# Two layers of a diffusion backbone: modulation weights requested on another queue, and a set order for norms and weight splits at the seam to the second layer

## The chip, the core and the metric

The kernel runs on one core of a Trainium2 chip. A core has five engines that work side by side, each through its own instructions in order: TensorE multiplies matrices (PE in the profile; its weight loads are PEld), VectorE (DVE) and ScalarE (ACT) work on elements, GpSimd (POOL) and SyncE (SP) here mostly request transfers between the chip's memory and the core's. A transfer is requested by an engine, in that engine's order, and moves on that engine's queue; sixteen DMA engines carry all queues. If an engine has to wait before it may request a transfer, because the buffer is still in use, what it would do next waits too.

The metric is the time of one execution on the device, in microseconds (us). Three runs of the kernel before gave 1735.34 to 1737.92 us, with a median of 1735.86.

## What is computed

Two layers work on 512 latent tokens and 256 context tokens of width 1024. Each layer modulates its normed input by six vectors that come from a conditioning vector c through a weight matrix, once for the latent and once for the context tokens:

```python
mx = jnp.split(c_act @ ada_w[i] + ada_b[i], 6, axis=-1)      # six vectors of 1024, layer i
h_x = modulate(rms_norm(x, norm1_g[i]), mx[0], mx[1])        # h * (1 + scale) + shift
# layer 0: windowed attention with a sink;  layer 1: retention in both directions
x = x + mx[2] * out_x
x = x + mx[5] * swiglu(modulate(rms_norm(x, norm2_g[i]), mx[3], mx[4]), ffn_w_in[i], ffn_w_out[i])
```

Here `swiglu` is `(silu(gate) * up) @ w_out` with a hidden width of 2816. The output is the latent stream. All data are float32; a product in that precision is made of three faster ones, from operands that are split into a high and a low part.

## The kernel before

**Splits.** Every operand of a product is split: ScalarE casts it to the high part (line L171), VectorE subtracts that from the operand to get the low part (L172). TensorE then does high by high, low by high and high by low. So each weight tile of 512 KB passes through one load, one cast of ScalarE and one subtraction of VectorE before TensorE can use it.

**Modulation tiles.** The six vectors of layer 1 aren't computed on TensorE. Each of 48 tiles of the transposed modulation weights (512 KB, buffer `adaw`, one buffer for layer 1) is loaded by `ada_load` (request at L275), multiplied with the row of c on VectorE and summed (`ada_tile`, L284; one such instruction for latent tokens alone, two where the context tokens need the vector too). `ada_next` does a tile and then requests the next, which therefore waits until VectorE is done with the buffer. Layer 1's tiles are requested by GpSimd, those eight of layer 0 that are handled so by SyncE (with three buffers).

**Layer 0's feed-forward part, gate and up.** From about 398 to 724 us, `seven(pos)` handles one of 20 blocks of 128 hidden units: seven products of 12 matmuls each by a scheme that saves an eighth product. SyncE requests the weights (`load_up` L1138 and L1139, `load_gate` L1134, `load_sum` L1143). After every second block `pair_sums` combines the activations and GpSimd stores them (`saved`, L1069 and L1071). GpSimd also requests transfers that add one part of a weight matrix to another in the chip's memory (`sum_add`, L830; `fo_sum`); `sum_copy` (L827, SyncE) comes before it. From block 5 on, two tiles are handled per block by `ada_next`, as the first and the third of the block's `jobs`.

**Layer 0's feed-forward part, output.** From about 724 to 889 us, seven products of six steps each (`FO`, 41 steps that TensorE does, the last two joined). Step i does 24 matmuls with two hidden blocks (12 in a product's last step). At its begin, `fo_split_weights(i + 2)` and `fo_split_tokens(i + 2)` split the operands of two steps later, and `fo_load(i + 3)` requests tokens (`op` from `saved`, L1227, 384 KB) and weights (`wraw` from `wfo` or `fo_sum`, L1234, 512 KB); three raw weight buffers go round, and three pairs of split ones. After a product `fo_add` (L1280) adds its sums to the streams. In the first five products, every even step ends with `ada_next`, for the 14 tiles that are left. In the last two products, squares for the next layer's norm are summed (`add_squares`, `context_square`, L1298; `context_total`, L1303), and in the last one `latent_norm` makes the first half of the latent tokens' normed input: per tile a multiply on VectorE (L1352), a cast with shift on ScalarE (L1355), and a low part on VectorE (L1356).

**Order.** In these two stages the order on all five engines is the program's, written by hand (`tc.manual_schedule`). From there on, in retention, a planner orders the work by its dependencies and costs; there `first_weights_v` requested and split the first two value weights (L1496, L171, L172), which `values_first` multiplies with the first half of the normed tokens (L1572), with `totals` between two halves of that product.

Of the kernel before, what the change touches and what calls it, by code (L numbers as in the profile page):

```python
# [54 lines left out]
def dit_kernel(ctx, tc, xT, cT, crow, small, consts, masks, tabs0, tabs1, jtab, adaQ, adaN, adaT, wst, wgu, wfo, out):  # L55
# [11 lines left out]
    def T(pool, cols, tag, bufs, dt=F32):  # L67
        return pool.tile([P, cols], dt, tag=tag, bufs=bufs, name=tag)
# [29 lines left out]
    def after(ins, others):  # L98
        for o in others if not by_hand[0] else ():
            tc.add_manual_dep(ins.ins, o.ins.name, order, reason="table set turn")  # L100
# [69 lines left out]
    def split(t, hi, lo, behind=()):  # L170
        after(nc.scalar.copy(hi, t), behind)  # L171
        return nc.vector.tensor_tensor(lo, t, hi, op=sub)  # L172
# [99 lines left out]

    def ada_load(l, part, d, room):
        w = T(room, 1024, "adaw", 1 if l else 3)
        (nc.gpsimd if l else nc.sync).dma_start(w, adaT[l, part * 8 + d])  # L275
        return w

    def ada_tile(l, part, d, streams, cr, behind, room, w=None):
# [970 lines left out]
    def fo_step(i, o, first, joined=False):  # L1249
        parts_, end = [], [fo.pop(j) for j in ((i, i + 1) if joined else (i,))]  # L1250
        k = 2 * FO[i][1]
        for x, w in end:
            n = x[0].shape[1] // 384
            for j in range(n):
                parts_.append((k, [t[:, j * 384:(j + 1) * 384] for t in x], w, j * 512))
                k += 1

        def one(k, xs, w, c, d):
            ws = slice(c + d * P, c + (d + 1) * P)
            for e, (p, r) in enumerate(((w[0], xs[0]), (w[1], xs[0]), (w[0], xs[1]))):  # L1260
                nc.tensor.matmul(o[d], p[:, ws], r, start=first and k + e == 0,  # L1261
                                 stop=k == PAIRS - 1 and e == 2, skip_group_check=True)

        if joined:
            for d in range(4):
                for part in parts_:
                    one(*part, d)
        else:
            for part in parts_:
                for d in range(4):  # L1270
                    one(*part, d)
# [71 lines left out]
    def first_quarters(k, half):  # L1343
        if k < 4:
            return h_first[k][:, 0:SC], h_first[k][:, SC:2 * SC]
        return [a[:, HALVES[half]] for a in h_rest[k - 4]]

    def latent_norm(half, ks, behind=()):
        b, y, c = mods[1, 0], ssq[0], HALVES[half]
        for k in ks:  # L1350
            t = hm[k][:, c]
            after(nc.vector.scalar_tensor_tensor(t, xr[k][:, c], acol[1, 0, 0][:, k:k + 1], y[:, c], mult, mult), behind)  # L1352
            if k > 3 or half == 0:
                hi, lo = first_quarters(k, half)
                nc.scalar.activation(hi, t, AF.Identity, bias=b[:, 0, k:k + 1])  # L1355
                nc.vector.scalar_tensor_tensor(lo, t, b[:, 0, k:k + 1], hi, add, sub)  # L1356

    def first_rms():
        tot = pj(SC)
# [13 lines left out]
    def late_sums(step):  # L1373
        if step < 2:
            add_squares(T0, (4 + 2 * step, 5 + 2 * step))
            for d in (4 + 2 * step, 5 + 2 * step):
                context_square(d, t_hn(SC))
        if step == 1:
            ctx_sum.append(pj(SC))
            context_total((4, 5), 4, 3)  # L1380
            first_rms()
        if step == 2:
            context_total((6, 7), 4, 3)
        if 0 < step < 5:
            latent_norm(0, (2 * step - 2, 2 * step - 1))

    def last_squares():
        y, c = ssq[0], slice(384, SX)
        for d in range(4):
            t = t_hn(512) if d < 2 else t_sq(512)  # L1390
            context_square(d, t[:, 0:SC])
            sq = t[:, SC:SC + P]
            nc.scalar.activation(sq, xr[d][:, c], AF.Square)
            nc.vector.tensor_tensor(y[:, c], y[:, c], sq, op=add)

    def nothing():
        pass
# [9 lines left out]
    def gates_negated():  # L1407
        ends.pop(0)()
        for s in range(2):
            nc.vector.tensor_scalar(mods[0, s][:, 0], mods[0, s][:, 5], -1.0, None, op0=mult)  # L1410

    row_t = []
    Hand = {mybir.EngineType.PE, mybir.EngineType.DVE, mybir.EngineType.Activation, mybir.EngineType.SP,
            mybir.EngineType.Pool}
    with tc.manual_schedule(engines=Hand):
        by_hand[0] = True
        for pos in range(2, FT):
            jobs = [nothing] * 3
            if pos == 2:
                jobs = [last_sum, gates_negated, nothing]  # L1420
            elif pos == 3:
                jobs[0] = rows_begin
            elif pos == 4:
                jobs[2] = rows_silu
                ada_ahead()
            else:
                cr = row_t[0]
                jobs[0] = jobs[2] = ada_next
            if pos == FT - 1:
                def begin():  # L1430
                    fo_split_weights(0)
                    fo_split_tokens(0)
                    fo_split_tokens(1)
                jobs[1] = begin
            end = seven(pos, jobs)
            for st in sum_turns.get(100 + pos, ()):
                st(None)
        fo_y = [bank("Y"), bank("Z"), bank("Z"), bank("Y")]
        o = fo_y
        for i, (prod, m) in enumerate(FO):  # L1440
            if m == 0 and prod:
                o = fo_y if prod in (2, 4) else fo_z if prod == 5 else [bank("X"), bank("X"), pj(384), pj(384)] \
                    if prod in (1, 3) else [bank("Y"), bank("Z"), bank("Z"), bank("Y")]
                if prod == 3:
                    fo_z = o
            if i == 0:
                fo_split_weights(1)
                last_gate(FT - 1)
            if i + 2 < len(FO):
                fo_split_weights(i + 2)  # L1450
                fo_split_tokens(i + 2)
                fo_load(i + 3)
            last = prod == 6 and m == (PAIRS - 3) // 2
            if i + 1 < len(FO) or last:
                fo_step(i, o, prod in (0, 1, 3, 6), last)
            if m == (PAIRS - 1) // 2:
                for args in (((0, 0),), ((0, 0),), ((4, 0, True),), ((4, 1),), ((4, 1, True), (0, 1)), ((4, 0),), ())[prod]:
                    fo_add(o, *args)
            if prod < 5:
                ada_next() if m % 2 == 0 and ada_q else None  # L1460
            elif prod == 5:
                early_sums(m)
            else:
                late_sums(m)
            if i == 2:
                Q.close()
                H = ExitStack()
                hpool[0] = H.enter_context(tc.tile_pool(name="hR", bufs=1, reuse_waits="tile", side="right"))
                h_rest += [(T(hpool[0], 512, "aq", 11, F32R), T(hpool[0], 512, "aq", 11, F32R)) for _ in range(4)]
                h_first += [T(hpool[0], 512, "aq", 11, F32R) for _ in range(3)]  # L1470
                off_grid(hpool[0], 16)
                h_first.insert(0, T(hpool[0], 512, "aq0", 1, F32R))
                hm += [T(hpool[0], 512, "qk", 8) for _ in range(KT)]
        fo_add(o, 0, 1)
        last_squares()
        by_hand[0] = False
    assert not ada_q
    F.close()
# [10 lines left out]
    hpool[1] = qp  # L1489
    off_grid(qp, 48)  # L1490
    h_sum = [(T(hS, 512, "sA", 16, F32R), T(hS, 512, "sA", 16, F32R)) for _ in range(KT)]
    chunk_base = wpos[0]

    def chunk(i, own=False):
        raw = T(qw, 1024, "wx", 4) if own else T(rp, 1024, "wraw", 2)
        nc.sync.dma_start(raw, wst[i])  # L1496
        return raw

    def add_chunk(raw, i):
        nc.gpsimd.dma_start(raw, wst[i], accum_op=add)  # L1500

    def split_chunk(raw, behind=()):
        w = w_parts(hpool[0])
        last_split[0] = split(raw, *w, behind)
        return w

    last_split, rope_end, rope_sum, other_sums = [None], [None], [None], []

    def t_qk(dt=F32R):
        return T(hpool[0], 512, "qk", 8, dt)  # L1510

# [125 lines left out]
        product_v(c, context_half(0), w, True)  # L1637
        return c

    wsel[0] = 2  # L1640
    b11 = first_weights_v(0)
    ends = []

    def totals():
# [8 lines left out]
    for hd in range(RH):  # L1653
# [2 lines left out]

        def other_values():

            b21 = [split_chunk(chunk(bv + i)) for i in (2, 3)]
            Xv = [W4("X"), W4("X")]  # L1660
            product_v(Xv, quarter_of("12"), b21, True)
            for t in range(2):
                nc.vector.tensor_tensor(vt[t], vt[t], Xv[t], op=add)
            c = cv if hd else context_values(b11)
            product_v(c, context_half(1), b21, False)
            vt.extend((T(rp, 512, "y0", 1), T(qp, 512, "vc", 1)))
            for t in range(2):
                nc.scalar.copy(vt[4 + t], c[t])
# [595 lines left out]
```

## Time and profile before

| | |
|---|---|
| median of 3 runs | 1735.86 us |
| profiled execution, whole time | 1735.32 us |
| its span, first to last instruction | 1733.2 us |
| mean granted TensorE clock | 0.991 |
| TensorE busy | 1685.6 us, 97% |
| VectorE busy | 1343.0 us, 77% |
| 48 tiles of layer 1, requested on GpSimd's queue | 512 KB each, median 4.0 us from request to landing |
| 8 tiles of layer 0, requested on SyncE's queue | 512 KB each, median 3.7 us |

A row of waits has the waiting engine, its tile and line, an arrow to what it waited for, and then the sum in us, the count and the longest. A row of instructions has its start, its length, engine, line, operation, written and read tiles with partitions and elements, and in brackets the idle time before it with what ended that. Rows of transfers have size and the time from request to landing. The clock is the share of full speed that TensorE was granted.

### The profile page before, as it was taken

Reading aid. Unit: us, or ns where it says so; the run is one execution under the profiler, and the core shown is the slowest. Engines: PE = TensorE matmul, PEld = TensorE weight load, DVE = VectorE, ACT = ScalarE, POOL = GpSimd, SP = SyncE. Lnnn points to the kernel's source line nnn. Section 1 sums busy time; section 2 is a strip of 40 time slices with the busy share of each in tenths; the row PEclk is TensorE's granted clock in tenths of the full one; section 3 lists DMA queues with packets and bytes.
Section 4 is the critical chain, followed back from the end, with each engine's and each line's share of the span. In section 5 each row is a group of like instructions: output and inputs, shape, how many; then the busy total and the mean of one; then the engine's idle time right before and its main releaser. Section 6 shows DMA issues by size and latency. Waiting matters only on the chain.

```text
span 1733.2 us, 27880 instructions
## 1 busy us (share of the span) xinstructions
PE 1685.6 (97%) x10798; PEld 1527.1 (88%) x10798; DVE 1343.0 (77%) x2395; ACT 895.0 (52%) x1565; POOL 116.2 (7%) x246
## 2 busy tenths in 40 slices
PE   8999999999989899999989999999999999999999
PEld 5878878899979899999978888888898899989998
DVE  6788888797768778877779866767757898876874
ACT  5578878474433343444565534534525565444442
POOL 0011111000111211200000000000000000000000
PEclk9999999999999999999999999999999999999999
DMA  9848967645766775798662644625624323333322
GB/s 384 310 90 188 238 145 192 212 152 173 218 211 227 226 234 197 273 314 288 234 176 62 183 110 100 189 65 125 193 62 110 122 74 107 114 109 107 102 86 85
DMA packets 113316, 293.87 MB, mean 170 GB/s; under 512 B 9520, under 2 KB 20288, under 8 KB 112928
## 3 DMA queue, kind: packets, MB, share of 16 engines
q1 hardware_dynamic: 87696, 218.75, 38.0%
q0 software_dynamic: 25200, 72.82, 17.7%
q8 instruction: 84, 1.38, 0.3%
q10 hardware_dynamic: 288, 0.52, 0.1%
q14 instruction: 48, 0.39, 0.1%
HBM read 274.82 MB, written 61.28 MB: 194 GB/s over the span
## 4 chain that ended last, share of the span: by engine, by line
PE 79%; DVE 8%; DMA 7%; ACT 3%; issue 2%; POOL 0%; SPq 0%; DVEq 0%; ACTq 0%
PE Y L971 13%; PE Z L1572 7%; PE Z L971 7%; PE pj L154 4%; PE pj L156 4%; PE pj L155 4%; PE X L971 3%; PE Y L1561 3%; DMA adaw<-in_adaT_dram 3%; PE S L727 2%; PE pT L753 2%; PE pO L775 2%; DVE wlo L172 2%; PE Z L1261 2%; PE Y L1261 2%; PE pj L1261 2%
## 5 line engine op out<-in xcount | busy, mean ns | idle before, releaser
L171 ACT CAST whi<-wraw 128x1024 fp32r<-128x1024 f32 (+1 forms) x285 | 295.8, 1042 | 303.1 <-PE Y L971 70.5
L172 DVE TENSOR_TENSOR wlo<-wraw,whi 128x1024 fp32r<-128x1024 f32 (+1 forms) x285 | 343.8, 1210 | 113.8 <-ACT whi L171 112.5
L971 PE MATMUL Y<-aq,whi 128*128 128x384 f32 x640 | 176.7, 342 | 0.0
L971 PE MATMUL Y<-aq,wlo 128*128 128x384 f32 x320 | 110.1, 344 | 19.9 <-DVE wlo L172 19.9
L971 PEld LDWEIGHTS Y<-aq,whi 128*128 128x128 f32 x640 | 120.0, 193 | 0.0
L284 DVE CUSTOM_DVE_ANT_0 y<-adaw,crow,small_sb 128x1024 bf16<-128x1024 f32 x64 | 82.1, 1283 | 45.7 <-DMA adaw<-in_adaT_dram 45.1
L1572 PE MATMUL Z<-whi,sA 128*128 128x512 f32 x256 | 80.7, 391 | 0.0
L971 PEld LDWEIGHTS Y<-aq,wlo 128*128 128x128 f32 x320 | 61.9, 194 | 21.1 <-DVE wlo L172 21.1
L108 ACT ACTIVATE pr<-pr,stat,qs 128x513 f32<-128x513 f32 (+2 forms) x96 | 74.3, 777 | 11.1 <-DVE stat L734 11.0
L154 PE MATMUL pj<-ax,whi 128*128 128x512 f32 x176 | 69.3, 394 | 0.7 <-DVE res L263 0.4
L156 PE MATMUL pj<-ax,whi 128*128 128x512 f32 x176 | 68.8, 391 | 0.0
L155 PE MATMUL pj<-ax,wlo 128*128 128x512 f32 x176 | 68.7, 390 | 0.0
L753 PE MATMUL pT<-const_sb,pr 128*128 128x128 f32 x352 | 56.4, 285 | 2.3 <-DVE pr L744 1.1
L263 DVE SCALAR_TENSOR_TENSOR res<-pj,mod,res 128x512 f32<-128x512 f32 (+1 forms) x64 | 45.3, 714 | 16.7 <-PE pj L156 16.7
L971 PE MATMUL Y<-sA,whi 128*128 128x256 f32 x304 | 58.1, 277 | 0.0
L728 DVE CUSTOM_DVE_ANT_0 pr<-S,mask,qs 128x256 f32<-128x256 f32 (+1 forms) x96 | 53.4, 568 | 5.4 <-PE S L727 4.4
L1572 PEld LDWEIGHTS Z<-whi,sA 128*128 128x128 f32 x256 | 48.0, 188 | 10.3
L971 PE MATMUL Y<-hx,whi 128*128 128x256 f32 x304 | 56.3, 277 | 0.0
L1261 PE MATMUL Y<-aq,whi 128*128 128x384 f32 x176 | 53.2, 338 | 2.0 <-ACT aq L171 2.0
L1572 PE MATMUL Z<-wlo,sA 128*128 128x512 f32 x128 | 50.5, 395 | 1.3 <-DVE wlo L172 1.3
L1261 PE MATMUL Z<-aq,whi 128*128 128x384 f32 x176 | 51.4, 334 | 0.0
L753 PEld LDWEIGHTS pT<-const_sb,pr 128*128 128x128 f32 x352 | 41.2, 145 | 11.2 <-issue 4.3
(598 smaller groups left out, 5102.6 us busy)
## 6 DMA issues: line engine op xcount, KB each, us to landing
wraw<-in_wst_dram SPq DMA_DIRECT2D x158, 512.0 KB, 3.7
adaw<-in_adaT_dram POOLq DMA_DIRECT2D x48, 512.0 KB, 4.0
op<-saved SPq DMA_DIRECT2D x35, 384.0 KB, 5.4
saved<-op POOLq DMA_DIRECT2D x33, 384.0 KB, 6.4
wraw<-in_wgu_dram SPq DMA_DIRECT2D x24, 512.0 KB, 4.5
gu_sum<-in_wgu_dram SPq DMA_DIRECT2D x8, 1280.0 KB, 12.7
gu_sum<-in_wgu_dram POOLq DMA_DIRECT2D x8, 1280.0 KB, 12.7
wraw<-fo_sum SPq DMA_DIRECT2D x20, 512.0 KB, 4.9
```

The lines of the kernel that those rows point to most:

```text
L108: ins = nc.scalar.activation(*args, **kw)
L154: nc.tensor.matmul(o, whi, xhi, start=first, stop=False)
L155: nc.tensor.matmul(o, wlo, xhi, start=False, stop=False)
L156: return nc.tensor.matmul(o, whi, xlo, start=False, stop=last)
L171: after(nc.scalar.copy(hi, t), behind)
L172: return nc.vector.tensor_tensor(lo, t, hi, op=sub)
L284: res.append(nc.vector.tensor_tensor_reduce(junk, w, cr[:, s * 1024:(s + 1) * 1024], 1.0, sm_t[:, C_ADAB + l * 48 + j:C_ADAB + l * 48 + j ...
L728: nc.vector.tensor_tensor_reduce(pt[:, c0:c0 + w], bank, mask[:, m0:m0 + w], 1.0, top, add, ALU.min, lo)
L753: nc.tensor.transpose(tp[:, a * P:(a + 1) * P], self.pr[(0, 2, 1, 3)[a]][:, ki * P:(ki + 1) * P], ident)
L971: nc.tensor.matmul(o, p, r, start=first and k + i == 0, stop=k == 3 and i == 2, skip_group_check=not first)
L1261: nc.tensor.matmul(o[d], p[:, ws], r, start=first and k + e == 0, stop=k == PAIRS - 1 and e == 2, skip_group_check=True)
L1572: ins = nc.tensor.matmul(os[t], p, r, start=first and k + i == 0, stop=k == 3 and i == 2, skip_group_check=by_k or not first)
```

## The change

Three things change; what is computed stays the same.

1. `ada_load` requests all tiles on SyncE's queue. In the program's order those 48 requests now stand among SyncE's loads.
2. In the last product, `latent_norm` begins a step later and takes three, three and two tiles in steps 2, 3 and 4 instead of two in each of steps 1 to 4. Within a group all multiplies come first, then all shifts on ScalarE, then all low parts.
3. Retention's first two value weights are requested and split inside the hand order: the first split before the last `fo_add`, the second after `last_squares`. The next two are ordered behind the last of these squares. The helpers `chunk`, `add_chunk` and `split_chunk` move up unchanged.

```diff
     def ada_load(l, part, d, room):
         w = T(room, 1024, "adaw", 1 if l else 3)
-        (nc.gpsimd if l else nc.sync).dma_start(w, adaT[l, part * 8 + d])
+        nc.sync.dma_start(w, adaT[l, part * 8 + d])
         return w
...
-    def latent_norm(half, ks, behind=()):
+    def latent_norm(half, ks, group=1):
         b, y, c = mods[1, 0], ssq[0], HALVES[half]
-        for k in ks:
-            t = hm[k][:, c]
-            after(nc.vector.scalar_tensor_tensor(t, xr[k][:, c], acol[1, 0, 0][:, k:k + 1], y[:, c], mult, mult), behind)
-            if k > 3 or half == 0:
-                hi, lo = first_quarters(k, half)
-                nc.scalar.activation(hi, t, AF.Identity, bias=b[:, 0, k:k + 1])
-                nc.vector.scalar_tensor_tensor(lo, t, b[:, 0, k:k + 1], hi, add, sub)
+        for k0 in range(0, len(ks), group):
+            some = ks[k0:k0 + group]
+            for k in some:
+                nc.vector.scalar_tensor_tensor(hm[k][:, c], xr[k][:, c], acol[1, 0, 0][:, k:k + 1], y[:, c], mult, mult)
+            some = [(k, *first_quarters(k, half)) for k in some if k > 3 or half == 0]
+            for k, hi, lo in some:
+                nc.scalar.activation(hi, hm[k][:, c], AF.Identity, bias=b[:, 0, k:k + 1])
+            for k, hi, lo in some:
+                nc.vector.scalar_tensor_tensor(lo, hm[k][:, c], b[:, 0, k:k + 1], hi, add, sub)
...
-        if 0 < step < 5:
-            latent_norm(0, (2 * step - 2, 2 * step - 1))
+        if step > 1:
+            latent_norm(0, ((0, 1, 2), (3, 4, 5), (6, 7))[step - 2], 3)
...
-            last = prod == 6 and m == (PAIRS - 3) // 2
-            if i + 1 < len(FO) or last:
-                fo_step(i, o, prod in (0, 1, 3, 6), last)
+            last = i == len(FO) - 2
+            fo_step(i, o, prod in (0, 1, 3, 6), last)
...
+            if last:
+                break
...
+        wsel[0] = 2
+        raws_v = [chunk(chunk_base + 4 + i) for i in range(2)]
+        b11.append(split_chunk(raws_v[0]))
         fo_add(o, 0, 1)
-        last_squares()
+        last_square = last_squares()
+        b11.append(split_chunk(raws_v[1]))
         by_hand[0] = False
...
-    wsel[0] = 2
-    b11 = first_weights_v(0)
...
-            b21 = [split_chunk(chunk(bv + i)) for i in (2, 3)]
+            b21 = [split_chunk(chunk(bv + i), [] if hd else [last_square]) for i in (2, 3)]
```

More of the change, by code (lines that the diff above doesn't have):

```diff
@@ L1393, in last_squares @@
             nc.scalar.activation(sq, xr[d][:, c], AF.Square)
-            nc.vector.tensor_tensor(y[:, c], y[:, c], sq, op=add)
+            ins = nc.vector.tensor_tensor(y[:, c], y[:, c], sq, op=add)
+        return ins
     def nothing():
@@ L1410, in gates_negated, with chunk, add_chunk, split_chunk @@
             nc.vector.tensor_scalar(mods[0, s][:, 0], mods[0, s][:, 5], -1.0, None, op0=mult)
+    def chunk(i, own=False):
+        raw = T(qw, 1024, "wx", 4) if own else T(rp, 1024, "wraw", 2)
+        nc.sync.dma_start(raw, wst[i])
+        return raw
+    def add_chunk(raw, i):
+        nc.gpsimd.dma_start(raw, wst[i], accum_op=add)
+    def split_chunk(raw, behind=()):
+        w = w_parts(hpool[0])
+        last_split[0] = split(raw, *w, behind)
+        return w
+    last_split, rope_end, rope_sum, other_sums = [None], [None], [None], []
+    chunk_base = wpos[0]
+    b11 = []
     row_t = []
@@ L1491, in dit_kernel @@
     h_sum = [(T(hS, 512, "sA", 16, F32R), T(hS, 512, "sA", 16, F32R)) for _ in range(KT)]
[L1492 to L1507, printed above, removed]
     def t_qk(dt=F32R):
```

## The prediction

> **What bounds the kernel now.** I read the page first, then waits and chain of 398 to 830 us, where the moved requests live, then the queues there.
>
> ```profile
> span 1733.2 us, 27880 instructions
> PE 1685.6 (97%) x10798; PEld 1527.1 (88%) x10798; DVE 1343.0 (77%) x2395; ACT 895.0 (52%) x1565; POOL 116.2 (7%) x246
> ```
>
> TensorE is busy for 97% of the span, so time can only come from its idle gaps and from matmuls at a lower clock. The waits of 398 to 830 us:
>
> ```profile
> POOL adaw L275 <- DVE mod L284: 301.1, 46, 16.0
> DVE y L284 <- DMA adaw<-in_adaT_dram: 45.1, 17, 8.0
> PE Y L971 <- DVE wlo L172: 19.9, 4, 5.4
> ```
>
> TensorE stands still four times, 19.9 us, each time for a weight split that VectorE does late. VectorE is late because a modulation tile lands late. The chain shows the first of the four with the slow matmuls after it (start, us, what; an undisturbed group of 12 last), and the table by stretches shows what the clock did over the whole stage (length, then busy us of TensorE, its weight loads, VectorE, ScalarE, GpSimd; granted clock):
>
> ```profile
> 470.36 12.25 DMA adaw<-in_adaT_dram
> 485.12 3.89 PE Y L971 x11
> 489.00 2.63 PE Z L971 x12
> ...
> 493.72 2.08 PE Z L971 x12
> ```
>
> ```profile
> 452.00:724.00 272.00, 252.13 (x1401) 250.85 (x1400) 210.72 (x314) 104.40 (x168) 44.77 (x70) 0.96 0.71 221
> 724.00:820.00 96.00, 96.00 (x555) 95.72 (x554) 74.08 (x100) 43.19 (x53) 9.73 (x18) 1.00 0.90 304
> ```
>
> After the gap, eleven matmuls took 3.89 us; at the undisturbed pace they take 11/12 x 2.08 = 1.91. Over the stage the clock was 0.96, and 4% of 252.1 busy us are 10.1 us (by the groups, 2.0 + 0.55 = 2.5 us behind this gap, four times 10). Gaps and slow matmuls together: 19.9 + 10.1 = **30 us**, all with one cause. GpSimd's queue names it:
>
> ```profile
> 462.01 1.18 POOL L830 DMA_DIRECT2D fo_sum<-in_wfo_dram  x1
> ...
> 470.36 0.56 POOL L275 DMA_DIRECT2D adaw<-in_adaT_dram  x1 [2.84 <-DVE mod L284]
> ```
>
> The tile requested at 470.36 stands behind an accumulating transfer (fo_sum) and four stores on the same queue; the accumulation alone needs 15.6 us to land (row below).
>
> **Part 1a, the 34 tiles of the gate and up stage: the gain.** In `seven`, SyncE's order becomes load_up, load_gate, tile, load_sum, tile. load_sum and load_up already wait for splits that VectorE does after the tile in question, so a tile's wait in front of them blocks nothing new; a request costs about 0.3 us of an idle sequencer. The four delays vanish if the tile gets past the accumulation. Against that stand the loads that were on SyncE's queue in the same stretch (requests from 462 to 464 us; and the last tile before the pile-up):
>
> ```profile
> fo_sum<-in_wfo_dram POOLq DMA_DIRECT2D x1, 1280.0 KB, 15.6
> adaw<-in_adaT_dram POOLq DMA_DIRECT2D x1, 512.0 KB, 3.8
> saved<-op POOLq DMA_DIRECT2D x1, 384.0 KB, 16.5
> wraw<-in_wgu_dram SPq DMA_DIRECT2D x1, 256.0 KB, 7.8
> wraw<-gu_sum SPq DMA_DIRECT2D x1, 256.0 KB, 10.4
> ```
>
> SyncE's loads got through during the accumulation, slowly: two halves of 256 KB by 7.8 and 10.4 us. VectorE's 8.0 us wait cost TensorE 5.4, so some 2.6 us of it is cover. A tile landing at 3.8 us costs nothing; one at 10.4 instead of 12.25 saves only 1.9 of a 5.4 us gap, and up to two thirds of the 30 stay. I take the near end, the full 30, for two reasons. GpSimd without the tiles in its order reaches stores and accumulation earlier; and a tile has rows of 1024 elements where these loads have 512, so at equal turns it moves twice the bytes. The Trainium skill, "DMA: Bandwidth & Descriptors", section "Queues, rings and completion order", says that each engine takes turns between queue rows packet by packet, and the 7.8 and 10.4 us loads that passed a 15.6 us one agree. The same page's "Rules for kernel authors" says against the change that all issuing engines share the same 16 engines, which is the second rival below.
>
> **Part 1b, the 14 tiles of the output stage: a new wait.** Here `fo_load` runs ahead on SyncE, held only by a free weight buffer:
>
> ```profile
> 787.08 1.23 DVE L172 TENSOR_TENSOR wlo<-wraw,whi 128x1024 fp32r<-128x1024 f32 x1 [3.43 <-ACT whi L171]
> 788.34 0.36 SPq L1234 DMA_DIRECT2D wraw<-fo_sum  x1
> SPq L1234 <- DVE wlo L172: 121.2, 41, 10.2
> SPq L275 <- DVE mod L284: 17.7, 5, 4.6
> ```
>
> The request goes out 0.03 us after the split that frees its buffer, three steps ahead of use. The last row is the eight tiles of layer 0, already on this queue: there SyncE itself stands still until VectorE has used the buffer, and everything behind stands too. With one `adaw` buffer, the same now happens in every even step. In program order after the tile of step i come: the request of the next tile, loads i+4 and i+5, and then the next tile's request, which waits for the tile of step i+2. That tile lies on VectorE behind split i+4, which needs load i+4. So a **loop** closes: tile used, request, token and weight loads behind it in one queue, split, tile. Its VectorE side:
>
> ```profile
> 800.55 1.05 ACT L171 CAST whi<-wraw 128x1024 fp32r<-128x1024 f32 x1 [2.36 <-PE pj L1261]
> ...
> 801.64 1.23 DVE L172 TENSOR_TENSOR wlo<-wraw,whi 128x1024 fp32r<-128x1024 f32 x1 [0.99 <-ACT whi L171]
> 802.78 0.95 DVE L172 TENSOR_TENSOR aq<-op,aq 128x768 fp32r<-128x768 f32 x1
> 803.65 1.28 DVE L284 CUSTOM_DVE_ANT_0 y<-adaw,crow,small_sb 128x1024 bf16<-128x1024 f32 x1
> 804.86 0.09 DVE L284 DVE_READ_ACCUMULATOR2_ANT mod<- 128x1 f32 x1
> ```
>
> From cast to released buffer: 804.95 - 800.55 = 4.4 us. The landing of three transfers in one queue (512, 384, 512 KB) is not in the trace; near it stand:
>
> ```profile
> adaw<-in_adaT_dram SPq DMA_DIRECT2D x8, 512.0 KB, 3.7
> wraw<-fo_sum SPq DMA_DIRECT2D x1, 512.0 KB, 3.9
> op<-saved SPq DMA_DIRECT2D x1, 384.0 KB, 4.5
> ```
>
> The last two were requested at 788.34 and 788.75, so the 384 KB behind the 512 landed 4.5 + 0.41 - 3.9 = 1.0 us later; 512 KB more are 1.0 x 512/384 = 1.35. Lower end: 3.7 + 1.0 + 1.35 = 6.05 us. Upper end: three transfers requested from 798.94 on over both queues, the last landing 800.23 + 5.7 = 805.9, so 7.0. I take 6.3, near the lower end because that one is a single queue, and the loop is 6.3 + 4.4 = **10.7 us** (10.45 to 11.4). By the Trainium skill, the same page, section "Anatomy of one DMA" (2.0 us plus the bytes at 436 GB/s), three transfers would be an estimated 5.3 us, the loop 9.7 and the end of the sum below 1728; but the single tile would be 3.2, where the row has 3.7.
>
> The loop runs 13 times. Two steps of TensorE take 8.3 us, or 6.2 across a product's half step, so it is longer than what it hides behind:
>
> ```profile
> 730.31 1.28 DVE L284 CUSTOM_DVE_ANT_0 y<-adaw,crow,small_sb 128x1024 bf16<-128x1024 f32 x1
> ...
> 826.53 1.28 DVE L284 CUSTOM_DVE_ANT_0 y<-adaw,crow,small_sb 128x1024 bf16<-128x1024 f32 x1
> 831.75 1.05 ACT L171 CAST whi<-wraw 128x1024 fp32r<-128x1024 f32 x1 [3.12 <-PE Y L1261]
> ```
>
> The first of the 14 tiles is done at 731.6, the last starts at 826.5, and step 28, which uses the split just before that last tile, begins at 831.75 (its start frees the buffer for this cast). With the loop the last tile is done at 731.6 + 13 x 10.7 = 870.7 and its split 1.3 earlier, 869.4: 37.7 us after 831.75. The 5.2 us of lead that VectorE has now are used up in that. Then loads run ahead again, but load 30 is only requested at 870.7; with 4.7 us of landing and 2.2 of split it comes some 2 us after steps 28 and 29 end. Loss: **40 us** (10.45: 36; 11.4: 49). Gaps of some 3 us per loop may lower the clock, but the loop doesn't pass through TensorE, so that costs it nothing.
>
> **Parts 2 and 3, the seam to retention.** TensorE's gaps there:
>
> ```profile
> 883.37 0.44 PE L1261 MATMUL Y<-aq,whi 128*128 128x384 f32 x1 [2.00 <-ACT aq L171]
> 893.90 1.35 PE L1303 MATMUL pj<-hn,ones_sb 128*128 128x256 f32 x4 [1.87 <-ACT hn L1298]
> 897.04 0.70 PE L227 MATMUL pj<-y,ones_sb 128*128 128x256 f32 x2 [0.49 <-DVE y L1394]
> ```
>
> The first is the last token split, which stands on ScalarE behind norms and retention's splits; with the norms one step later and in threes it goes ahead. The second and third are squares behind splits that the scheduler had put first; the set order puts the second weight's split after them. The count of norm instructions doesn't change; three shifts in a row let VectorE stop waiting for ScalarE between them. The gain is at most the three gaps, 4.4 us, with little clock; at least -3, if the second weight's split (1.05 + 1.23 us, now behind the squares) is what TensorE waits for and the free scheduling behind it falls less well. I take **4**, near the upper end, because split and sums of squares run side by side.
>
> **The sum**, against the profiled execution's 1735.3 us (span 1733.2 and 2.1 around it; the median of the runs, 1735.9, is the same to 0.03%): 1735.3 - 30 - 4 + 40 = **1741 us**. Own range: loss 36 to 49, gains in the near case 27 to 34: 1737 to 1757 at the ends; a landing under the lower end's 6.05 us is not excluded, so 1733 to 1752 is what I hold likely.
>
> **Rivals.** (1) *The loop doesn't bind*: SyncE's loads keep enough lead. For it: TensorE now has no gap between 724 and 820 us (the stretch's row above), and loads go three steps ahead. Against it: the layer 0 row above, SyncE held by such a request. Time 1735.3 - 34 = 1701; a loop of 8.5 us, half hidden, gives 731.6 + 13 x 8.5 - 1.3 - 831.75 = 8 us of loss, 1709. The loop costs anything only where it is longer than 7.4 us, the mean spacing of the tiles now ((826.5 - 730.3)/13), plus its share of the lead; it outweighs the gains of 34 from about 10.2 us on, so under that the kernel is faster. (2) *The tiles stay late in the gate and up stage*, since the same 16 engines carry the accumulation: at 10.4 us of landing some 20 of the 30 us stay, 1761. For it: the 7.8 and 10.4 us. Against it: the turns argued above. (3) That the request doesn't move is excluded: the line of `ada_load` is the only one that issues it.
>
> **How the numbers follow.** A measurement of this kernel can't tell less than 0.2%, 3.5 us, from no change. Forecast, a binding loop with part 1a's gain: 0.62, of which three quarters lie over 1739.4, a fifth within 3.5 us and the rest below. Rival (1): 0.24, faster. Rival (2): 0.14, slower. Faster 0.24 + 0.04 = 0.28; same 0.13; slower 0.45 + 0.14 = 0.59. The range 1706 to 1758 holds the forecast's 0.62 and about half of each rival, some 0.8; the likeliest case's own is 1733 to 1752.
>
> **What would show it.** Right: no wait of TensorE at L971 between 452 and 724 us and no modulation tile landing over 8 us; SyncE waiting at L275 for VectorE's tiles; between 724 and some 900 us ScalarE's casts at L171 released by the weight transfers, not by TensorE, and the 13 tile spacings near 10.7 us; the seam's gaps at L1261 and L1303 gone. Wrong: tile spacings still near 7.4 us with casts released by TensorE (rival 1), or tiles landing at 10 us and gaps at L971 still there (rival 2).

## The result and the profile after

The change makes the kernel **slower**: 1760.6 us (median; 1755.3 to 1761.5) against 1736.9 for the kernel before, measured beside it, a ratio of 1.0129 (95% interval 1.0104 to 1.0153). The direction was forecast, the size was not: 1741 us, with a range up to 1758.

The stages show two large terms of opposite sign. Each block has one row for the gate and up stage (it begins at 402 us) and one for the output stage; in the block of before, the output stage's row comes first. A row has the stretch, its length, the busy us of TensorE, weight loads, VectorE, ScalarE and GpSimd with their instructions, then granted clock, DMA share and GB/s. Before:

```profile
723.00:889.00 166.00, 163.59 (x936) 161.95 (x936) 127.33 (x187) 82.43 (x112) 10.48 (x20) 1.00 0.77 256
...
402.00:723.00 321.00, 301.13 (x1691) 299.67 (x1683) 245.51 (x373) 128.25 (x208) 48.69 (x75) 0.96 0.69 220
```

After:

```profile
402.00:699.70 297.70, 294.20 (x1683) 292.74 (x1683) 244.41 (x372) 127.89 (x207) 31.04 (x43) 0.99 0.75 232
699.70:911.00 211.30, 188.18 (x936) 178.25 (x935) 126.75 (x193) 80.88 (x114) 2.60 (x6) 0.90 0.60 201
```

The gate and up stage went from 321 to 298 us, its clock from 0.96 to 0.99. The output stage went from 166 to 211 us with the same 936 matmuls; VectorE and ScalarE did the same work in it, TensorE stood idle for 23 us and ran at a clock of 0.90, and the transfers moved 201 GB/s instead of 256: nothing is short there, things wait for each other. In the output stage before, ScalarE's casts of weights waited for TensorE:

```profile
ACT whi L171 <- PE Y L1261: 38.2, 19, 3.1
...
ACT whi L171 <- PE pj L1261: 31.3, 16, 3.1
```

The waits after the change, of SyncE's queue and then of all engines, from the end of gate and up on:

```profile
SPq L275 <- DVE mod L284: 97.5, 14, 8.0
```

```profile
ACT whi L171 <- DMA wraw<-fo_sum: 71.9, 13, 8.8
ACT whi L171 <- DMA wraw<-in_wfo_dram: 35.4, 8, 8.9
...
PE X L1261 <- ACT aq L171: 10.6, 4, 4.1
...
PE Y L1261 <- ACT aq L171: 8.0, 4, 2.7
```

SyncE stands for 97.5 us at the tile's request (L275) until VectorE has used the buffer; the weights behind it land late, so ScalarE's casts wait 107 us for transfers; TensorE waits for the casts. That is the loop that the prediction describes. One turn of it, in SyncE's requests, the landings of the first and the third of them, and VectorE's work:

```profile
753.57 0.33 SPq L275 DMA_DIRECT2D adaw<-in_adaT_dram  x1
753.99 0.39 SPq L1227 DMA_DIRECT2D op<-saved  x1
754.46 0.42 SPq L1234 DMA_DIRECT2D wraw<-fo_sum  x1
...
764.92 0.34 SPq L275 DMA_DIRECT2D adaw<-in_adaT_dram  x1
```

```profile
adaw<-in_adaT_dram SPq DMA_DIRECT2D x1, 512.0 KB, 3.6
wraw<-fo_sum SPq DMA_DIRECT2D x1, 512.0 KB, 6.0
```

```profile
761.60 1.23 DVE L172 TENSOR_TENSOR wlo<-wraw,whi 128x1024 fp32r<-128x1024 f32 x1 [6.99 <-ACT whi L171]
762.74 0.95 DVE L172 TENSOR_TENSOR aq<-op,aq 128x768 fp32r<-128x768 f32 x1
763.61 1.28 DVE L284 CUSTOM_DVE_ANT_0 y<-adaw,crow,small_sb 128x1024 bf16<-128x1024 f32 x1
764.81 0.08 DVE L284 DVE_READ_ACCUMULATOR2_ANT mod<- 128x1 f32 x1
```

Request of the tile at 753.57, weights landed at 754.46 + 6.0 = 760.5, VectorE idle for 7 us, then split, split, tile, and the next request at 764.92: a turn of 11.35 us. Over the 13 turns these weights land 6.2 to 7.5 us after the tile's request, 6.9 in the mean. Over the stage, the first and the last of the 14 tiles:

```profile
706.90 1.28 DVE L284 CUSTOM_DVE_ANT_0 y<-adaw,crow,small_sb 128x1024 bf16<-128x1024 f32 x1
```

```profile
854.85 1.28 DVE L284 CUSTOM_DVE_ANT_0 y<-adaw,crow,small_sb 128x1024 bf16<-128x1024 f32 x1
```

13 turns take 148.0 us, 11.4 each, where the tiles came every 7.4 us before.

### The profile page after: what moved, and what is told of

Same layout as the page of the kernel before. It is cut to its first block, busy times and chain, and to the rows that moved or that the text cites. A ratio compares the mean times of both kernels' runs of the same rounds, so it can differ in the third digit from the quotient of the medians.

```text
span 1759.2 us, 27878 instructions
## 1 busy us (share of the span) xinstructions
PE 1705.5 (97%) x10798; PEld 1538.0 (87%) x10798; DVE 1339.9 (76%) x2395; ACT 892.0 (51%) x1565; POOL 90.4 (5%) x198
## 4 chain that ended last, share of the span: by engine, by line
PE 71%; DMA 10%; DVE 10%; issue 4%; ACT 4%; SPq 1%; POOL 0%; DVEq 0%; ACTq 0%; POOLq 0%
PE Y L971 12%; PE Z L1580 6%; PE Z L971 6%; PE pj L154 4%; PE pj L156 4%; PE pj L155 4%; DMA wraw<-fo_sum 3%; DMA wraw<-in_wst_dram 3%; PE Y L1569 3%; PE X L971 3%; PE S L727 2%; PE pT L753 2%; DVE wlo L172 2%; PE pO L775 2%; PE pj L1580 2%
## 5 line engine op out<-in xcount | busy, mean ns | idle before, releaser
L171 ACT CAST whi<-wraw 128x1024 fp32r<-128x1024 f32 (+1 forms) x285 | 295.5, 1041 | 366.0 <-DMA wraw<-fo_sum 71.9
L971 PE MATMUL Y<-aq,whi 128*128 128x384 f32 x640 | 173.5, 336 | 0.0
L971 PEld LDWEIGHTS Y<-aq,whi 128*128 128x128 f32 x640 | 117.5, 189 | 0.0
L971 PE MATMUL Y<-aq,wlo 128*128 128x384 f32 x320 | 108.1, 338 | 3.5 <-DVE wlo L172 3.5
L1261 PE MATMUL Y<-aq,whi 128*128 128x384 f32 x176 | 57.9, 364 | 10.1 <-ACT aq L171 8.0
L971 PEld LDWEIGHTS Y<-aq,wlo 128*128 128x128 f32 x320 | 60.6, 189 | 4.8 <-DVE wlo L172 4.8
L971 PE MATMUL Y<-sA,whi 128*128 128x256 f32 x304 | 58.1, 277 | 0.0
L263 DVE SCALAR_TENSOR_TENSOR res<-pj,mod,res 128x512 f32<-128x512 f32 (+1 forms) x64 | 45.3, 714 | 16.5 <-PE pj L156 16.5
L971 PE MATMUL Y<-hx,whi 128*128 128x256 f32 x304 | 56.3, 277 | 0.0
L1261 PE MATMUL X<-aq,whi 128*128 128x384 f32 x132 | 43.6, 373 | 12.1 <-ACT aq L171 10.6
L1261 PE MATMUL Z<-aq,whi 128*128 128x384 f32 x176 | 55.0, 356 | 0.0
```

The lines of the kernel that those rows point to most:

```text
L971: nc.tensor.matmul(o, p, r, start=first and k + i == 0, stop=k == 3 and i == 2, skip_group_check=not first)
```

## The experiments

The stages below are measured between starts: gate and up from its first matmul in `seven` to the first of the output products (L1261 before), output from there to the first of retention (L1572), seam from there to the first scores of head 0, and the rest from there to the end of the span. The stages are in us and from one profiled execution of each kernel, the medians from all its runs. y4 and y5 leave out some sums and so compute something else; they only show what those sums cost.

| kernel | median | ratio to before (95%) | gate, up | output | seam | rest |
|---|---|---|---|---|---|---|
| before | 1735.9 to 1737.2 | | 320.9 | 166.0 | 67.5 | 776.6 |
| after | 1760.6 | 1.0129 (1.0104 to 1.0153) | 297.7 | 211.4 | 68.9 | 779.1 |
| x1 tiles alone | 1757.4 | 1.0123 (1.0108 to 1.0139) | 297.8 | 216.6 | 66.9 | 774.6 |
| x2 seam alone | 1735.0 | 0.9992 (0.9983 to 1.0002) | 321.2 | 163.2 | 68.6 | 777.7 |
| x3 tiles by stage | 1709.9 | 0.9861 (0.9836 to 0.9886) | 297.4 | 166.0 | 67.0 | 775.1 |
| x4 loads ahead | 1711.3 | 0.9859 (0.9828 to 0.9889) | 300.1 | 163.2 | 67.4 | 776.1 |
| z1 one step ahead | 1711.4 | 0.9854 (0.9837 to 0.9871) | 301.1 | 164.9 | 67.8 | 778.7 |
| z2 half the tiles | 1740.0 | 1.0017 (0.9998 to 1.0037) | 294.7 | 191.6 | 66.5 | 775.5 |
| y4 no adds | 1705.2 | 0.9823 (0.9808 to 0.9837) | 291.4 | 167.5 | 66.6 | 776.0 |
| y5 no second sums | 1704.6 | 0.9817 (0.9803 to 0.9832) | 292.3 | 163.8 | 66.4 | 776.8 |
| y3 norms only | 1708.4 | 0.9835 (0.9820 to 0.9850) | 296.3 | 163.2 | 66.0 | 778.4 |
| y2 both splits first | 1703.7 | 0.9820 (0.9802 to 0.9838) | 295.4 | 163.2 | 64.4 | 776.1 |

**Which part makes the loss.** x1 is the kernel before with the queue of the tiles changed and nothing else; x2 has the other two parts alone (the request as before):

```diff
-        (nc.gpsimd if l else nc.sync).dma_start(w, adaT[l, part * 8 + d])      # x1
+        nc.sync.dma_start(w, adaT[l, part * 8 + d])
```

> The kernel before with part 1 alone (every tile on SyncE's queue). If the request loop of the output stage makes the loss and the seam's two parts little: output stage 45 to 48 us longer than before, gate and up stage 23 us shorter, in all 1757 to 1762 us. If the set order of norms and splits at the seam carries part of the loss, this kernel comes out below 1755.

> Parts 2 and 3 alone; layer 1's tiles stay on GpSimd's queue. My forecast was 4 us faster than before, 1733. What the trace after the change shows (3.9 us won between the output stage's end and the first rotated product, 5.2 us lost behind it) would give about 1 us slower or no change, 1735 to 1739. If the seam carries part of the loss: over 1742.

Part 1 alone gives the whole loss: 1757.4 us, with 23 us won in the gate and up stage and 50.6 lost in the output stage, 2.6 more than the most that I had expected. Parts 2 and 3 together are no change, 0.9992; the 4 us that I had given them are not there.

**Which place makes it.** x3 leaves the tiles of the output stage on GpSimd's queue, all but the first of the 14, which is requested ahead of it:

```diff
-        (nc.gpsimd if l else nc.sync).dma_start(w, adaT[l, part * 8 + d])
+        (nc.gpsimd if l and ada_late[0] else nc.sync).dma_start(w, adaT[l, part * 8 + d])
...
         o = fo_y
+        ada_late[0] = True                                   # ahead of the output stage
```

> The kernel before, with the 34 tiles of the gate and up stage on SyncE's queue and the 14 of the output stage still on GpSimd's. If the loss comes from the request loop of the output stage alone, the gain of 23 us in the gate and up stage stays and the output stage takes its 166 us: 1710 to 1717 us. If moving a request costs the same at every place, or the gain is paid back later: above 1725.

1709.9 us: the gain of the first stage stays, the output stage has its 166.0 us back. The same line moves a request at both places; at one it gains 23 us, at the other it costs 50.

**Is it the loop, or the queue?** x3 also takes the tiles' bytes off SyncE's queue, so it doesn't tell these apart. x4 keeps every transfer of the kernel after on its queue and changes only the order: ahead of the wait for a tile, the loads of two more steps are requested.

```diff
-                fo_load(i + 3)
+                load_to(i + 3)                               # fo_load of every step up to i + 3 not yet loaded
...
-                ada_next() if m % 2 == 0 and ada_q else None
+                if m % 2 == 0 and ada_q:
+                    load_to(i + 5)
+                    ada_next()
```

> The kernel after, with the token and weight loads of two more steps requested before the wait for the tile instead of behind it; the same transfers on the same queue. If the loop (tile used, request, loads behind it, split, tile) is the cause, the output stage falls from 211 us to 166 to 172 and the kernel to 1713 to 1722 us. If the queue's share of the DMA engines, or the tiles' bytes on it, is the cause, the order changes little: above 1745.

The output stage takes 163.2 us and the kernel 1711.3, both some 2 us under what I had expected. In x4's waits of the output stage, ScalarE's casts wait for TensorE again, not for transfers:

```profile
ACT whi L171 <- PE pj L1261: 30.4, 16, 3.1
...
ACT whi L171 <- PE Y L1261: 26.8, 13, 3.1
...
ACT whi L171 <- DMA wraw<-in_wfo_dram: 11.8, 5, 4.3
```

The queue carries the same bytes in the same stage, so neither the queue nor its share of the engines was the cause. The loop was, as far as its order goes: shown by this run against the one after the change.

**Which load closes the loop, and what one turn costs.** z1 requests one step ahead instead of two (`load_to(i + 4)`). z2 is x1 with only the first 7 of the 13 requests of the output stage on SyncE's queue:

```diff
-        (nc.gpsimd if l else nc.sync).dma_start(w, adaT[l, part * 8 + d])
+        (nc.gpsimd if l and len(ada_q) < 7 else nc.sync).dma_start(w, adaT[l, part * 8 + d])
```

> The kernel after, with the loads of one more step (not two) requested ahead of the wait for the tile. In the loop it is the first load behind the request that the next split, and through it the next tile, waits for; the second is used a step later. If that is right, one step is enough: output stage 163 to 168 us, in all 1708 to 1717 us, as with two. If SyncE's standing still as such is the cause, half of the 45 us should come back: over 1725.

> The kernel before, with the 34 tiles of the gate and up stage and the first 7 of the 13 later requests on SyncE's queue, the last 6 on GpSimd's. If each request costs one loop of 11.4 us in place of 7.4, and the lead of 5.2 us is used up once: 7 loops make 80 us, the eighth tile starts 24 us later than without, and the kernel takes 1733 to 1740 us. If the loss is a single event at the stage's begin, all of it is there: 1752 or more; if it comes from the last loops, none: about 1711.

One step is enough: 164.9 us. SyncE still waits for the tiles there, 45.0 us in all, and it costs little (1.7 us against x4's 163.2), since the load that the next split needs is out already. And the cost goes by turns: seven of them add 25.6 us to the output stage (191.6 against 166.0), thirteen 50.6. These are single executions, z2's the fastest of its seven (1732.7 to 1744.7 us), x1's the slowest of its four. By the medians z2 lies 30 us above x3 and x1 47.5. So z2 has part of the loss, neither all nor none, and a single event at one end of the stage is excluded; the cost of one turn is 3.7 to 4.3 us by these figures and not known more closely.

**What the stalls in the gate and up stage were.** y4 is the kernel before without the four accumulating transfers of `fo_sum`'s second half; y5 is x4 without these and with plain copies of all four parts, all of them requested by block 3, ahead of the first tile (x4 has them after blocks 3, 9 and 13):

```diff
-    spread(fo_steps(1), (103, 103, 105, 107, 109, 111, 113, 115))
+    spread([fo_steps(1)[j] for j in (0, 1, 4, 6)], (103, 103, 109, 113))     # y4: no sum_add
```

> The kernel before without the four accumulating transfers of the second half of the output weights' sums (left out: those sums are then not formed). If these transfers, ahead of the tiles on GpSimd's queue, make the four stalls, the gate and up stage falls from 321 us to about 291 to 293 and the kernel to 1705 to 1708 us. If the four stores per pair suffice for a stall, at least two of the four gaps of 5 us stay: above 1718.

> The kernel with loads ahead, without the four accumulating transfers and with plain copies of all four parts requested early (left out: the second half's sums). With the change the gate and up stage still takes 298 to 300 us where 20 blocks of 14.56 us are 291. If the rest is what those transfers and the copies between them, now on the tiles' own queue, still cost, it falls to 291 to 293 us. If it is the tiles themselves on SyncE's queue, it stays at 297 or more.

Without the accumulations, and with the tiles still on GpSimd's queue, the stage has no gap and the full clock. Stretch of y4, and from the answers for the buffer `adaw` of y4, of before and of after, the landings of the tiles requested from 440 us on (least, median, most us):

```profile
402.00:693.50 291.50, 291.50 (x1690) 291.34 (x1683) 245.76 (x373) 128.05 (x208) 43.68 (x71) 1.00 0.68 224
```

```profile
DMA to landing us min/median/max: 3.7/4.2/6.0
```

```profile
DMA to landing us min/median/max: 3.7/4.0/12.3
```

```profile
DMA to landing us min/median/max: 3.4/4.1/10.0
```

So the four accumulations were the one cause of the 30 us: 320.9 - 291.4 = 29.5. The change to SyncE's queue takes the tiles past them only in part: 10.0 us at most instead of 12.3, and some 6 us are left in the stage, which y5 removes (292.3). Two things can hold tiles up on that queue: the accumulation itself, and the copies between accumulations (L827), which SyncE requests. The traces have both. In y5, with no accumulation at all, the very first tile (430.14) is requested right behind two copies and takes 15.5 us; it isn't needed so soon. After the change, a tile requested at 469.87, during an accumulation and with no copy near, landed after 7.2 us, and TensorE had no gap behind it. The tile of 10.0 us was requested at 528.43; a copy had been on the queue from 519.93 to 527.97, three loads requested behind it were still under way, and an accumulation began at 528.52. Behind this tile is the one long gap that is left, 2.8 us. No run separates the share of the two.

**The seam.** Parts 2 and 3 shorten the output stage's last product by 2.8 us (163.2 against 166.0) and seem to lengthen the seam by about 1 (x2: 68.6; after: 68.9; before: 67.5). The seam scatters as much: kernels with the changed order have 66.4 to 68.9 us there, those with the planner's 66.0 to 67.5. y3 is x4 without part 3; y2 is x4 with both first weights split before the last gated add:

```diff
-        b11.append(split_chunk(raws_v[0]))
+        b11 += [split_chunk(raw) for raw in raws_v]                              # y2
         fo_add(o, 0, 1)
         last_square = last_squares()
-        b11.append(split_chunk(raws_v[1]))
```

> The kernel with loads ahead, without part 3: the first weights are split where the planner puts them, as before the change; parts 1 and 2 stay. If part 2 alone makes the output stage's last product shorter (166 to 163 us), that stays, and the stretch behind the first rotated product is back at 40 us: 1704 to 1709 us. If the shorter last product needs the set order of the splits too, the output stage is back at 166 us: 1709 to 1713.

> The kernel with loads ahead, and both of retention's first weights split before the last gated add, so the squares come after both. If the late second split (its raw buffer is free late, so a later weight's load is late) makes the 5 us that are lost between the first rotated product and the first scores (45.3 us with the change, 39.8 before), that stretch falls to 40 to 42 us; a gap of some 2 us may come back ahead of it. In all 1706 to 1711 us. If the stretch is long because the planner got other work, it stays at 44 to 46 us.

y3 keeps the 163.2 us, so these come from part 2 alone. In y2 the seam falls from 67.4 to 64.4 us. The "stretch behind the first rotated product" of the expectation, 45.3 us in x4, is 40.2 in y2; but that stretch held 285 matmuls in x4 and 266 in y2, so part of its length was work that had moved behind the mark, and the whole seam is the measure. SyncE's requests for retention's weights, x4 first, then y2:

```profile
846.98 16.93 SPq L1417 DMA_DIRECT2D wraw<-in_wst_dram  x3
865.38 0.90 SPq L1417 DMA_DIRECT2D wx<-in_wst_dram  x2
868.77 1.46 SPq L1417 DMA_DIRECT2D wraw<-in_wst_dram  x2
```

```profile
842.92 18.05 SPq L1417 DMA_DIRECT2D wraw<-in_wst_dram  x4
861.50 0.91 SPq L1417 DMA_DIRECT2D wx<-in_wst_dram  x2
```

```profile
PE X L1589 <- ACT whi L171: 2.2, 1, 2.2
```

In x4 only three weights are requested ahead of the `wx` loads; the fourth must wait for the raw buffer that the late second split holds, is requested at 868.77 behind 1 MB of other loads, and TensorE waits 2.2 us for its cast (last row, x4's waits; y2 has no such wait). In y2 all four are out before. Of the kernels that compute the whole, y2 has the lowest median: 1703.7 us, 0.9820 of before, and under the 1706 to 1711 that I had expected. Its profiled span is 7.2 us shorter than x4's, of which 4.7 lie in the gate and up stage, which scatters between runs, and 3.0 in the seam, where it is 2 us under the lowest of the kernels with the change's order. Its interval (0.9802 to 0.9838) overlaps those of x4 and y3, so that it is the fastest is not shown.

## Why the prediction was wrong

By its own steps, in profiled executions (1761.0 against 1735.3 us, 25.7 more; the spans 25.9):

- **Part 1a, the gain of 30 us: 23.2.** What the stalls cost was right (29.5 by y4), and that GpSimd's queue held the tiles up. What failed is the choice of the near end, that a tile on the other queue lands in time: one took 10.0 us, and TensorE still waited 3.5 us at L971. Both reasons given held only in part. GpSimd did request earlier, the first accumulation at 438.15 instead of 462.01, where no tile was late for it, but three more came among the tiles. And the tile of 512 KB did move faster than a 256 KB load of the same time (10.0 and 8.8 us), but not in time. The copies on SyncE's own queue were not considered at all. The truth lay between the ends. By "Rules for kernel authors" in the Trainium skill's "DMA: Bandwidth & Descriptors", the second rival's ground, spreading transfers over the issuing engines doesn't help bandwidth, because all run on the same 16 DMA engines; here the other queue bought 23.2 of 29.5 us, so the rule fits at most the 6 that are left.
- **Part 1b, the loss of 40 us: 48 to 51.** Place, mechanism and count were right: 13 turns, SyncE held at L275, the weights late, the lead used up once. The term that was mis-sized is the landing of three transfers in one queue: 6.3 us was taken between 6.05 and 7.0, and 6.9 was measured. In the means of the 13 turns the tile took 3.8 us (3.7 in the sum of the lower end), the tokens behind it 1.1 more (1.0), and the weights behind those 1.95 more, where the sum scaled the tokens' 1.0 by size to 1.35; why this third step is longer stays open. VectorE's side was 4.4 us as forecast. With 11.4 for 10.7 the same sum gives 40 + 13 x 0.7 = 49 us; x1 has 50.6, and the kernel after 45.4 with the 2.8 that part 2 gives back. The lower clock of 0.90 adds nothing on top, as forecast: the turns alone make up the loss. The estimate from "Anatomy of one DMA" on the same page of the Trainium skill, 5.3 us for the three and a turn of 9.7, was further off; the fit there is measured for transfers that GpSimd issues, and these are SyncE's.
- **Parts 2 and 3, a gain of 4 us: about none** (0.9992, x2; 2.8 less 1.4 at the seam in the kernel after). Part 2 gave the 2.8. Part 3 closed the gaps at L1303 and L227 and opened others behind them (the longest in x2 2.3 us, for a cast at L171); the step that failed is to go by "split and sums of squares run side by side" alone: the raw buffer that the late split holds was not looked at, nor the load that waits for it.
- **The rest**, 776.6 to 779.1 us, was taken as unchanged; other kernels of the table have 774.6 to 778.7 there without a change to it, so nothing is read from it.

All four differences go the same way: 7 + 8 + 2.6 + 2.5, some 20 us over the forecast's 1741. The range's upper end was drawn from the loop's upper end with part 1a's gain full; it should have held the loop's upper end together with the second rival in part. That the measured 1760.6 is the second rival's 1761 is chance: that rival kept the loop at 40 us and 20 of the 30 us of stalls, the runs have 48 and 6. Rival (1), that the loop doesn't bind, is refuted by the tile spacing of 11.4 us and by x4, where only the order differs. (Its example of a loop of 8.5 us adds up to 9 us of loss, not 8; nothing else rests on it.)

## What to carry to other kernels

A request that must wait for a buffer is not a cheap line on an idle queue: count what stands behind it in its engine's order, and ask whether the thing it waits for needs one of those. If so a loop closes, and its length is landing time of everything up to that load plus the work up to the release; compare that with the spacing it has now. Request first what can go at once, then what has to wait: one step of order was worth 46 us of the output stage here (211.4 against z1's 164.9), on the same queue with the same transfers.

## What was not expected of the hardware

Of three transfers of 512, 384 and 512 KB requested back to back on one queue the last landed after 6.9 us, the mean of 13 turns, although the first took 3.8 and the second 1.1 more; the sum from single differences, 6.05, was 0.85 us too short, most of it in the third. And with four accumulating transfers of 1280 KB gone, a stage that had moved 220 GB/s on average lost all its stalls, while its share of busy DMA engines hardly changed (0.69 to 0.68): it was their 14 to 16 us at one place, not the mean load, that made tiles late.
